# Interleaving the recurrent-gate quarters with the gate-branch products of a two-block kernel

## Chip, cores and metric

The kernel runs on one NeuronCore of a Trainium2 chip. The metric is the device time of one execution in microseconds (us).

## The reference

Two transformer-like blocks run one after the other over 256 tokens of width 1024. The change sits in the second block, in its recurrent branch. Cut to that branch, the second block computes:

```
xn = rmsnorm(x, norm_mix)
u_rnn, u_gate, q, k_c, v_c, ..., g_a, g_b = split(xn @ w_in)
xc = causal_depthwise_conv(u_rnn)                      # 1344 channels, 4 taps
r = sigmoid(block_diag(xc, w_a) + b_a)                 # 4 blocks of 336 channels
i = sigmoid(block_diag(xc, w_x) + b_x)
a = exp(-8 * r * softplus(-lam));  u = sqrt(1 - a^2) * (i * xc)
h_t = a_t * h_{t-1} + u_t                              # scan over tokens
y_a = h * gelu(u_gate)
y_b = sparse attention over q, k_*, v_*
h = x + (sigmoid(g_a) * (y_a @ proj_a) + sigmoid(g_b) * (y_b @ proj_b)) @ w_out
out = h + relu(rmsnorm(h) @ w_mlp_in)^2 @ w_mlp_out
```

All of it is in float32 precision: every weight and every activation is split into a high and a low part, and each product is made of three matmuls (high by high, high by low, low by high).

## The kernel before

**Products.** `ws` (L304 on) makes one product of 256 output channels by 256 tokens. Its weights come in two halves through `wload` (L284): one DMA from the SP queue into a `raw` tile (4 buffers), a cast on ScalarE (`whi`, L298, 3 buffers) and a subtraction on VectorE (`wlo`, L266, called from there, 3 buffers). Each half feeds 24 matmuls of 128x256, so a product has 48. It accumulates in one PSUM bank of the pool `acc`, which has 4 banks, and the bank is free again when the product's `sink` function has read it. `as_` (L327 on) makes products with tokens on the partitions: two banks, four weight pieces.

**The recurrent branch.** `block2` runs five products of `u_rnn` (`sink_u`) and one of the two 64-channel ends (`sink_t`). Each sink runs the four-tap convolution on VectorE (L1132 to L1135) and writes its 256 channels to a scratch tensor `sx` in HBM (L1142, L1147). The scratch is there because the convolution lies in rows of 128 channels and the block-diagonal gates want rows of 112: the quarters `xr` (3 rows of 112, 336 channels) are read back from `sx` (L1156). Both transfers are issued from ScalarE's queue.

Then `NY = 1` product of `u_gate` (`sink_ug`, L1151) is traced, and then the four gate quarters in a loop. A quarter splits `xr` (L274 on ScalarE, L275 on VectorE), loads two block-diagonal weights (`gate_a`, `gate_x`, each 112x1008), runs 54 matmuls into 3 banks, and passes the result through tanh, exp and tanh on ScalarE (L1177, L1179, L1184, L1186), a square on GpSimd (L1185), and short operations on VectorE (L1178, L1180, L1187). The other four products of `u_gate` follow the loop, then two products of the merge gates (`sink_g`, L1197, L1198).

After that comes the recurrence's tail: one square root over all 12 rows (L1201), a table load and a gelu over `u_gate`'s result (L1203), 12 multiplications (L1206) and 12 scans (L1207) on VectorE. The result is written to a scratch `sh` and read back in rows of 128 (L1209, L1215), multiplied (L1216) and split (L274, L275).

**The attention that follows** takes its tiles from pools that lie where the recurrent branch's pools (`rn`, `rn2`) lay. Its first product pair (`sink_c`, L1252 and L1253, two banks) writes the tile `zc`, and its first `as_` product (`sink_q`, two banks) comes behind.

**Order.** The kernel is scheduled by a list scheduler: each engine's queue is put in order before the run, by a timing model of its own and, among what that model holds ready, by the order in which the program was traced. On the chip each engine's queue then runs strictly in that order, and a transfer issued from ScalarE's queue waits there for what it reads.

Of the kernel before, what the change touches and what calls it, by code (L numbers as in the profile page):

```python
# [21 lines left out]
P = 128  # L22
T = 256
# [12 lines left out]
RW = 112  # L36
RC = 12
D_RNN = 1344
NX = 11
NH2 = 16  # L40
# [9 lines left out]
BG, BGH = 4, 5  # L50
KR = 2
NG1 = 2
NY = 1
RQ = lambda nc: nc.scalar
NL = 3
CHUNKS = (256, 256, 256, 128, 128)
# [8 lines left out]
FLEN = 512  # L65
# [153 lines left out]
class Kern:  # L219
# [875 lines left out]
    def block2(self):  # L1095
        nc, tc, a, cp = self.nc, self.tc, self.a, self.cp
        vec = self.vec
        w_in = ("w_in_2", 0)
        act = self.act_h
# [9 lines left out]
        HK = p1.tile([P, NH2, T], F32, name="HK")  # L1109
# [6 lines left out]
        with tc.tile_pool(name="rn", bufs=1) as rp, tc.tile_pool(name="rn2", bufs=2) as r2:  # L1116
# [3 lines left out]
            xr = rp.tile([RW, RC, T], F32, name="xr")  # L1120
# [7 lines left out]
            sx, sh = (self.dr.tile([D_RNN, T], F32, name=nm) for nm in ("sx", "sh"))  # L1128
# [9 lines left out]
            def sink_u(c, ps):  # L1138
                c *= 2
                for i in range(2):  # L1140
                    conv(c + i, P, ps[:, i])
                RQ(nc).dma_start(sx[c * P:(c + 2) * P].rearrange("(c p) t -> p c t", p=P), xc[:, c:c + 2, :])  # L1142

            def sink_t(c, ps):

                conv(NX - 1, half, ps[:half, 0])
                RQ(nc).dma_start(sx[(NX - 1) * P:D_RNN], xc[:half, NX - 1, :])  # L1147
                nc.vector.tensor_tensor(yg[half:, NX - 1, :], ps[half:, 0], rB[half:], op=ALU.mult)

            def sink_ug(c, ps):  # L1150
                nc.vector.tensor_tensor(yg[:, 2 * c:2 * c + 2, :], ps, rB2, op=ALU.mult)  # L1151
            for i in range(5):
                self.ws(w_in, 256 * i, 256, P, act, sink_u)
            self.ws(w_in, 0, 2 * half, P, act, sink_t, nkp=8, col="ends")
            for b in range(4):
                RQ(nc).dma_start(xr[:, 3 * b:3 * b + 3, :], sx[336 * b:336 * (b + 1)].rearrange("(c p) t -> p c t", p=RW))  # L1156
            for i in range(NY):
                self.ws(w_in, 256 * i, 256, P, act, sink_ug, base=D_RNN)
            nc.sync.dma_start(HK, bass.AP(tensor=self.scr.tensor, offset=self.scr.offset, ap=[[1, P], [FLEN, NH2], [1, T]]))
            for b in range(4):  # L1160
                xh = r2.tile([RW, 3, T], F32R, tag="xh", name=self.n("xh"))
                xl = r2.tile([RW, 3, T], F32R, tag="xl", name=self.n("xl"))
# [4 lines left out]
                for o in range(3):  # L1167
                    c = 3 * b + o
# [17 lines left out]
                nc.scalar.activation(W2[:, bs, :], W2[:, bs, :], AF.Tanh)  # L1186
                nc.vector.scalar_tensor_tensor(W2[:, bs, :], a2, 1.0, W2[:, bs, :], op0=ALU.add, op1=ALU.mult)  # L1187

            for i in range(NY, 5):
                self.ws(w_in, 256 * i, 256, P, act, sink_ug, base=D_RNN)  # L1190

            gate_out = [self.h8().rearrange("p (c t) -> p c t", c=8)]

# [17 lines left out]
            for c in range(0, NX, 2):  # L1211
                n = 2 if c < NX - 1 else 1
# [334 lines left out]
```

## Time and profile before

| What | Value |
|---|---|
| median of 3 runs | 1906.32 us (1904.04 to 1907.57) |
| profiled execution | 1909.29 us, of which the span is 1907.2 us |
| TensorE busy | 1614.0 us, 85% of the span |
| VectorE busy | 854.8 us, 45% |
| ScalarE busy | 577.0 us, 30% |
| recurrent branch of the second block | from about 1341 to 1456 us of the span |

The profiled execution is one run and 3.0 us above the median; 2.0 us of it lie outside its span. Times in the rows are microseconds from the start of the span.

### The profile page before, as it was taken

To read this page: it belongs to the slowest core of one execution; us is meant where nothing else is said; L and a number is where in the kernel's file an instruction comes from. 1 tells how busy PE (TensorE), PEld (TensorE's weight loads), DVE (VectorE), ACT (ScalarE), POOL (GpSimd) and SP (SyncE) were. 2 spreads that over 40 slices of the span, in tenths; PEclk is the share of its full clock that TensorE was granted. 3 is DMA by queue.
4 is the path that set the end of the run, shared out by engine and by line. 5 is a ranking of instruction groups with operands and counts; after the bars stand their busy time and mean duration, and the time that the engine had idled before them with its cause. 6 is when DMAs were issued, how large, how long until landed. Compare 5 with 4: busy or idle time off the path is not lost. (4 is left out here: it accounts for less than half of the span.)

```text
span 1907.2 us, 27940 instructions
## 1 busy us (share of the span) xinstructions
PE 1614.0 (85%) x11259; PEld 1082.4 (57%) x11259; DVE 854.8 (45%) x1760; ACT 577.0 (30%) x1033; POOL 60.1 (3%) x74
## 2 busy tenths in 40 slices
PE   8998887765667899988867766778999999999999
PEld 8898431221213698984311211136998788679987
DVE  7987220111001389862100110014888656556643
ACT  4455110001001345551100010014474445445532
POOL 0100000000000011000000000000011100000000
PEclk9999898887888999998988878789999999889999
DMA  7658899999999765598999999996657632226554
GB/s 281 226 176 302 334 425 427 426 425 425 426 427 426 299 249 187 178 330 351 426 426 427 424 427 426 427 425 257 203 172 251 203 112 91 80 89 189 196 190 133
DMA packets 109725, 567.27 MB, mean 297 GB/s; under 512 B 12107, under 2 KB 21259, under 8 KB 61713
## 3 DMA queue, kind: packets, MB, share of 16 engines
q1 hardware_dynamic: 102976, 558.45, 75.7%
q10 hardware_dynamic: 5984, 5.82, 1.0%
q8 instruction: 93, 1.52, 0.3%
q0 software_dynamic: 624, 1.09, 0.2%
q14 instruction: 48, 0.39, 0.1%
HBM read 561.48 MB, written 3.83 MB: 296 GB/s over the span
## 5 line engine op out<-in xcount | busy, mean ns | idle before, releaser
L261 PE MATMUL ps<-mw,h 128*32 128x512 f32 x2032 | 314.1, 718 | 139.7 <-DMA mw<-in_w_exp_up_dram 72.4
L266 DVE TENSOR_TENSOR wlo<-raw,whi 128x1024 fp32r<-128x1024 f32 (+3 forms) x286 | 343.5, 1203 | 187.6 <-ACT whi L298 180.0
L298 ACT CAST whi<-raw 128x1024 fp32r<-128x1024 f32 (+3 forms) x286 | 294.8, 1033 | 433.6 <-PE ps L261 211.3
L261 PE MATMUL ps<-h,whi 128*128 128x256 f32 x2208 | 295.0, 283 | 9.4 <-ACT h L407 6.3
L261 PEld LDWEIGHTS ps<-h,whi 128*128 128x128 f32 x2208 | 274.1, 190 | 15.7 <-ACT h L407 7.8
L261 PEld LDWEIGHTS ps<-mw,h 128*32 128x32 f32 x2032 | 50.0, 118 | 342.0 <-DMA mw<-in_w_exp_up_dram 164.5
L261 PE MATMUL ps<-mw,mw 128*32 128x512 f32 (+3 forms) x1584 | 145.4, 469 | 45.7 <-DMA mw<-in_w_exp_down_dram 40.1
L261 PE MATMUL ps<-h,wlo 128*128 128x256 f32 x1104 | 153.2, 280 | 0.5 <-DVE wlo L266 0.5
L261 PEld LDWEIGHTS ps<-h,wlo 128*128 128x128 f32 x1104 | 139.3, 188 | 1.2 <-DVE wlo L266 0.7
L904 DVE TENSOR_TENSOR x<-x,ps 128x512 f32<-128x512 f32 (+2 forms) x60 | 34.6, 581 | 225.7 <-PE ps L261 225.7
L839 ACT ACTIVATE mw<-ps 128x512 f32<-128x512 f32 x16 | 9.5, 597 | 399.4 <-PE ps L261 394.8
L840 DVE TENSOR_TENSOR mw<-mw,ps 128x512 f32<-128x512 f32 x16 | 11.0, 688 | 264.0 <-issue 139.6
L261 PEld LDWEIGHTS ps<-mw,mw 128*32 128x32 f32 (+1 forms) x1584 | 46.9, 115 | 128.9 <-DMA mw<-in_w_exp_down_dram 76.1
L501 DVE SCALAR_TENSOR_TENSOR mw<-mw,vec,mw 128x256 f32<-128x256 f32 x240 | 111.0, 508 | 0.0
L261 PE MATMUL ps<-whi,h 128*128 128x512 f32 (+1 forms) x512 | 104.0, 345 | 0.0
L261 PE MATMUL ps<-mw 128*128 128x512 f32 (+4 forms) x328 | 91.0, 446 | 14.8 <-ACT mw L898 14.3
L812 DVE TENSOR_TENSOR h<-ps,vec 128x256 f32<-128x256 f32 (+1 forms) x80 | 29.6, 371 | 161.4 <-PE ps L261 161.3
L261 PEld LDWEIGHTS ps<-h,h 128*128 128x128 f32 x512 | 68.3, 206 | 58.8 <-issue 52.0
L261 PEld LDWEIGHTS ps<-whi,h 128*128 128x128 f32 x512 | 78.9, 190 | 16.2 <-issue 3.8
L261 PE MATMUL ps<-h,h 128*128 128x128 f32 x512 | 78.7, 300 | 9.4 <-DVE h L800 9.4
L898 ACT COPY mw<-ps 128x512 f32<-128x512 f32 (+2 forms) x50 | 21.6, 431 | 205.3 <-PE ps L261 205.3
L261 PEld LDWEIGHTS ps<-mw 128*128 128x128 f32 (+1 forms) x328 | 46.1, 197 | 60.7 <-ACT mw L898 35.5
(338 smaller groups left out, 1809.7 us busy)
## 6 DMA issues: line engine op xcount, KB each, us to landing
mw<-in_w_exp_gate_dram SPq DMA_DIRECT2D x128, 1024.0 KB, 19.6
mw<-in_w_exp_up_dram SPq DMA_DIRECT2D x126, 1024.0 KB, 19.6
mw<-in_w_exp_down_dram SPq DMA_DIRECT2D x118, 1024.0 KB, 19.6
raw<-in_w_in_dram SPq DMA_DIRECT2D x129, 512.0 KB, 4.4
raw<-in_w_mlp_in_dram SPq DMA_DIRECT2D x32, 512.0 KB, 3.5
raw<-in_w_mlp_out_dram SPq DMA_DIRECT2D x32, 512.0 KB, 3.5
raw<-in_w_out_dram SPq DMA_DIRECT2D x24, 512.0 KB, 4.4
raw<-in_w_ple_gate_dram SPq DMA_DIRECT2D x16, 512.0 KB, 16.5
```

What stands on the lines that cost most here:

```text
L261: return self.nc.tensor.matmul(out, lhsT, rhs, start=start, stop=stop)
L266: self.nc.vector.tensor_tensor(lo, src, hi.bitcast(F32), op=ALU.subtract)
L298: nc.scalar.copy(hv, raw[ps, :n])
L501: nc.vector.scalar_tensor_tensor(cacc[:, c, :], u[:, c, j:j + T], vec[:, wc + j:wc + j + 1], cacc[:, c, :], op0=ALU.mult, op1=ALU.add)
L812: nc.vector.tensor_tensor(xg[:, k:k + n, :], ps[:, :n * P].rearrange("p (k s) -> p k s", k=n), self.vec[:, gcol + k:gcol + k + n].unsqueez ...
L839: nc.scalar.activation(sg, G, AF.Silu)
L840: nc.vector.tensor_tensor(sg, sg, U, op=ALU.mult)
L898: nc.scalar.copy(ys[i], Y[:, :dw])
L904: nc.vector.tensor_tensor(xs, xs, pc[:, :dw], op=ALU.add)
```

## The change

The constant `NY` goes. The read of a quarter of `xr` from `sx` moves from behind all six `u_rnn` products into a function `fetch`, which the sinks call: a quarter's read is traced right after the write that completes its 336 channels. In front of the first gate quarter stand two products of `u_gate` in place of one, and one more is traced behind each of the first three quarters; none follows the loop. The read of the position bias `HK` is traced ahead of these products and no longer behind the first. The number of products, matmuls, transfers and other instructions is the same.

```diff
-NY = 1
@@
                 RQ(nc).dma_start(sx[c * P:(c + 2) * P].rearrange("(c p) t -> p c t", p=P), xc[:, c:c + 2, :])
+                fetch((c + 2) * P)
+
+            def fetch(n):
+
+                while len(xps) < 4 and (len(xps) + 1) * 336 <= n:
+                    b = len(xps)
+                    RQ(nc).dma_start(xr[:, 3 * b:3 * b + 3, :], sx[336 * b:336 * (b + 1)].rearrange("(c p) t -> p c t", p=RW))
+                    xps.append(None)
@@
                 RQ(nc).dma_start(sx[(NX - 1) * P:D_RNN], xc[:half, NX - 1, :])
+                fetch(D_RNN)
@@
+            xps = []
             for i in range(5):
                 self.ws(w_in, 256 * i, 256, P, act, sink_u)
             self.ws(w_in, 0, 2 * half, P, act, sink_t, nkp=8, col="ends")
-            for b in range(4):
-                RQ(nc).dma_start(xr[:, 3 * b:3 * b + 3, :], sx[336 * b:336 * (b + 1)].rearrange("(c p) t -> p c t", p=RW))
-            for i in range(NY):
+            nc.sync.dma_start(HK, bass.AP(tensor=self.scr.tensor, offset=self.scr.offset, ap=[[1, P], [FLEN, NH2], [1, T]]))
+            for i in range(2):
                 self.ws(w_in, 256 * i, 256, P, act, sink_ug, base=D_RNN)
-            nc.sync.dma_start(HK, bass.AP(tensor=self.scr.tensor, offset=self.scr.offset, ap=[[1, P], [FLEN, NH2], [1, T]]))
             for b in range(4):
...
                 nc.vector.scalar_tensor_tensor(W2[:, bs, :], a2, 1.0, W2[:, bs, :], op0=ALU.add, op1=ALU.mult)
 
-            for i in range(NY, 5):
-                self.ws(w_in, 256 * i, 256, P, act, sink_ug, base=D_RNN)
+                if b < 3:
+                    self.ws(w_in, 256 * (b + 2), 256, P, act, sink_ug, base=D_RNN)
```

## Rows read from the trace of the kernel before

**Rows 1.** Page, part 1: busy us, share of the span, instructions of each engine.

```profile
PE 1614.0 (85%) x11259; PEld 1082.4 (57%) x11259; DVE 854.8 (45%) x1760; ACT 577.0 (30%) x1033; POOL 60.1 (3%) x74
```

**Rows 2.** Stages: length; busy us and instructions of PE, PEld, DVE, ACT, POOL; clock; DMA.

```profile
1372.90:1376.00 3.10, 0.04 (x1) 0.00 (x0) 2.74 (x6) 0.83 (x1) 0.00 (x0) 1.00 0.70 183
1376.00:1380.20 4.20, 3.78 (x18) 3.56 (x19) 3.37 (x5) 2.73 (x3) 0.00 (x0) 0.60 0.54 160
1391.00:1396.00 5.00, 3.32 (x26) 2.89 (x25) 3.17 (x4) 4.99 (x9) 1.47 (x1) 1.00 0.73 222
1406.80:1436.00 29.20, 29.20 (x249) 29.13 (x248) 27.93 (x45) 18.43 (x21) 3.64 (x2) 1.00 0.64 198
1372.90:1463.90 91.00, 84.55 (x645) 81.04 (x645) 82.41 (x127) 60.15 (x78) 9.73 (x10) 0.98 0.67 209
1419.80:1463.90 44.10, 43.24 (x320) 40.81 (x319) 41.98 (x63) 23.01 (x25) 3.12 (x6) 1.00 0.74 237
1466.00:1556.00 90.00, 90.00 (x568) 70.19 (x568) 57.63 (x129) 37.72 (x51) 11.26 (x9) 1.00 0.58 185
```

**Rows 3.** Waits of PE, 1338 to 1446: total us, times, longest.

```profile
PE ps L261 <- ACT xh L274: 3.1, 1, 3.1
PE ps L261 <- DVE wlo L266: 1.7, 2, 1.2
PE ps L261 <- ACT whi L298: 1.2, 3, 0.5
PE ps L261 <- DVE xl L275: 0.8, 2, 0.4
```

**Rows 4.** Timeline of PE: start, us, line, operands, count, idle before and releaser.

```profile
1371.84 1.10 PE L261 MATMUL ps<-h,wlo 128*128 128x256 f32 x8
...
1406.80 2.05 PE L261 MATMUL ps<-h,whi 128*128 128x256 f32 x16
...
1465.52 0.61 PE L261 MATMUL ps<-raw,zp 128*60 128x256 f32 x2 [0.48 <-PE ps L261]
```

**Rows 5.** Timeline of ACT and its queue (ACTq) around the first two quarters.

```profile
1363.94 0.38 ACTq L1142 DMA_DIRECT2D sx<-W  x1
...
1368.32 0.34 ACTq L1156 DMA_DIRECT2D xr<-sx  x1
...
1375.15 0.83 ACT L274 CAST xh<-xr 112x768 fp32r<-112x768 f32 x1 [4.91 <-DMA xr<-sx]
...
1377.73 1.03 ACT L298 CAST whi<-raw 112x1008 fp32r<-112x1008 f32 x1
1379.74 0.33 ACTq L1156 DMA_DIRECT2D xr<-sx  x1
1383.39 0.84 ACT L274 CAST xh<-xr 112x768 fp32r<-112x768 f32 x1 [4.63 <-DMA xr<-sx]
```

**Rows 6.** Timeline of the last quarter's way into the tail, ACT and DVE.

```profile
1411.99 0.85 ACT L1184 ACTIVATE Aa<-W 112x768 f32<-112x768 f32 x1 [0.50 <-DVE W L1178]
...
1416.91 2.77 ACT L1201 ACTIVATE W<-W 112x3072 f32<-112x3072 f32 x1
...
1419.86 2.77 DVE L1206 TENSOR_TENSOR ur<-ur,W 112x256 f32<-112x256 f32 x8
```

**Rows 7.** DVE's groups by line, 1419.8 to 1463.88: count, busy us, mean ns, idle before.

```profile
L266 DVE TENSOR_TENSOR wlo<-raw,whi 128x1024 fp32r<-128x1024 f32 x14 | 16.9, 1215 | 0.4 <-ACT whi L298 0.3
...
L1197 DVE TENSOR_TENSOR h<-ps,rB 128x512 f32<-128x512 f32 x2 | 1.4, 684 | 0.0
L1151 DVE TENSOR_TENSOR yg<-ps,rB 128x512 f32<-128x512 f32 x2 | 1.3, 670 | 0.0
```

**Rows 8.** Timeline of POOL and DVE where the attention's first tile is written.

```profile
1456.18 0.11 POOL L1246 MEMSET s<- 64x8 f32 x1 [41.44 <-DVE ya L275]
...
1462.57 1.30 DVE L1253 TENSOR_TENSOR s<-ps,rB 64x510 f32<-64x510 f32 x2
```

**Rows 9.** Timeline of the SP queue at the start of the recurrent branch.

```profile
1340.16 0.38 SPq L1159 DMA_DIRECT2D HK<-scr  x1
```

## The prediction

> **What bounds the kernel now.** I read the page first, then the stages around the change, then who TensorE waited for, then the queues one by one. The page says that TensorE is busy for 85% of the span [rows 1], so time is won where it stands still. The table of stages shows two such places in the recurrent gates: from 1372.9 to 1376.0 it does nothing, and from 1391 to 1396 it is busy for 3.32 of 5 us [rows 2]. The list of waits gives the sum: 3.1 us for `xh`, the first quarter's cast, and 1.7, 1.2 and 0.8 us for `wlo`, `whi` and `xl`, together 6.8 us [rows 3]. The first stand costs more than itself. Behind it the granted clock is 0.60 for 4.2 us, a mix of 1.2 and 2.4 GHz, and 18 matmuls ran [rows 2]; at the 0.117 us that one takes in the undisturbed stage (29.20 us for 249, [rows 2]) they are 2.1 us of work, and with the 0.4 us of standing in it the clock cost 1.7 us. What the change aims at is so 6.8 + 1.7 = 8.5 us, 0.45% of the span.
>
> The cause of the first stand is a round trip: the second `sx` write is issued at 1363.94, the read of quarter 1 at 1368.32, and its cast starts at 1375.15, 4.91 us after ScalarE was free for it [rows 5]. TensorE ended the one free product at 1371.84 + 1.10 = 1372.9 [rows 4].
>
> The Trainium skill, DMA: Bandwidth & Descriptors, section "Anatomy of one DMA — SWDGE (gpsimd) path", fits a transfer as 2.0 us and its bytes at 436 GB/s; an estimate by that page is 2.6 us for the write and 2.8 us for the read, so that quarter 1 would be there at 1369.3, before the free product ends, and there would be no stand to remove. The page's fit is for another issuing engine, this trace has 4.4 and 6.8 us, and the trace decides.
>
> **The change part by part.**
>
> *The reads of `xr`.* In the trace the first two reads stand already between the `sx` writes, not behind the last one [rows 5]: the scheduler had hoisted them to the moment their channels are written. Tracing them earlier gives them rank over casts, but nothing is ready sooner, since each waits for the convolution and the write before it. I take 0. Behind each read, ScalarE's casts are queued; a read put ahead of one cast more would hold it as the second one did, at most the 4.63 us of idle before the second `xh` [rows 5]. That is a rival below.
>
> *`HK`.* Its read is moved past two weight loads on the SP queue, but it is issued at 1340.16 already [rows 9], 33 us before TensorE ends the free product behind which it was traced. Cost 0 on either side: two loads that it might now hold up are needed 26 us later.
>
> *The second free product.* 48 matmuls by 0.117 us are 5.6 us, so TensorE is busy until 1378.5, past the 1375.15 at which the first quarter is there. The 3.1 us and the clock's 1.7 us go. What is late next is the quarter's own weights: there are 3 `whi` buffers, the second product now takes the two that `gate_a` and `gate_x` had, and ScalarE stands at `xh` until 1376.0. The next cast in its queue ran from 1377.73 to 1378.8 [rows 5], and the subtraction behind takes 1.2 us [rows 7], so the first low part is there at about 1380.0 and TensorE waits 1.2 us (it can do two matmuls of high parts before). Bounds: 0, if the cast goes ahead of the small gelu, and the rival's 5.4 us.
>
> *One product behind each of the first three quarters.* A quarter has 54 matmuls, 6.3 us of TensorE. ScalarE was busy for 4.99 of 5 us where TensorE waited from 1391 to 1396 [rows 2]: a quarter alone fills it. A product between gives it 5.6 us with two casts in them, so I let the 0.5 + 1.2 us of waits there go, and the small ones for `xl` as well; bounded by 0 and their 2.9 us in all.
>
> *What moves back: the last quarter.* Before, TensorE ended it at 1406.8 and four `u_gate` products followed [rows 4]. Now all stand ahead: 1372.9 + 4 x 5.63 + 4 x 6.33 + 1.2 = 1422.0. The tail needs the square root over all rows, hence the last quarter. From the last matmul to the first multiplication of the tail it took 1419.86 - 1406.80 = 13.1 us before, of which the part from exp on took 7.9 us [rows 4, 6]. The rest was ScalarE's arrears, which the mixing takes away. Between 8.7 us (7.9 and a tanh and a VectorE step) and 13.1 us I take 9, by the near end: the tail starts at about 1431 and not at 1419.9, 11 us later.
>
> *What waits for the tail.* The attention's first tile is cleared at 1456.18, after the last split of `ya`, for which GpSimd had stood 41.44 us [rows 8]: the attention's pools lie on the recurrent branch's and open when its last reader is done. Until then `sink_c` cannot empty its two banks, nor `sink_q` its two, and `acc` has four. Behind the first `as_` product TensorE has no bank. Before this was just in time: `sink_c` ended at 1463.87 [rows 8] and the next matmuls began at 1465.52, 0.48 us late [rows 4].
>
> VectorE does that stretch almost without a gap (27.93 of 29.20 us up to 1436, 41.98 of 44.10 us from the tail's start to the end of `sink_c`, [rows 2]). In these 1463.87 - 1419.86 = 44.0 us it did, beside the tail, 14 `wlo`, 2 `L1151` and 2 `L1197` [rows 7]. In the changed order TensorE is in the second `sink_g` product when the tail starts, so that 7 `wlo`, both `L1151` and one `L1197` are already done: 7 x 1.21 + 2 x 0.67 + 0.68 = 10.5 us, taken as 10, since neighbours overlap a little. So `sink_c` ends at 1431 + 34 = 1465.0, and with the 1.65 us that lay between, TensorE goes on at 1466.7 and not at 1465.5. **Sum: +1.2 us.** TensorE's work from 1431 to there is about 25 us out of 36: the 8.5 us that are saved in the gates come back as standing at the full banks or for `wlo` behind the scans, which are traced ahead of the `sink_c` products and so outrank their weights. A long stand may bring the slow clock again, up to 1.7 us; inside a stretch that VectorE sets it is hidden, so 0. From 1466 to 1556 TensorE is busy for 90.00 of 90 us [rows 2], and what is won or lost is kept.
>
> Bounds of the sum: no gap on VectorE (2.1 us were in the 44) and no late cast -2.1 us; ScalarE's arrears as before +4.1, the clock +1.7. The profiled execution of 1909.29 us would be 1910.5; against the median of 1906.32, **1907.5 us**, own range 1905 to 1914.
>
> **The rivals.**
>
> *The gates' gain is kept.* If the tail does not set the end, TensorE loses only the 1.2 us: -8.5 + 1.2 = -7.3, so 1899. For it: VectorE stands for 91.00 - 82.41 = 8.6 us between 1372.9 and 1463.9 [rows 2], and gelu can now run before the tail. Against it: 3 buffers stop `wlo` from running ahead, and the tail starts 11 us later. The Trainium skill, Perfetto Trace Analysis, section "Optimization Strategy" says that regimes bound by different engines may gain from being interleaved; that is this rival, and the trace bears it out for ScalarE in the gates only. A part of the gain, 4 us, is counted here.
>
> *ScalarE's queue stands at the second quarter (slower).* The second `xh` stood right behind one cast and the second read, and waited until 1383.39 [rows 5]. With a product more ahead of the quarters, the cast of the first quarter's second weight comes behind that `xh`, if the scheduler's model has quarter 2 early. Then it ends at 1385.3 and its low part at 1386.5; TensorE runs out at about 1381 and stands for 5.4 us. The last quarter, the tail and the banks all come that much later: +6.6, so 1912.9. It decides as soon as that one cast stands behind the second `xh`. For it: in the trace the second `xh` precedes even the first quarter's tanh. Against it: the cast is traced earlier and wins if both are ready.
>
> *The change does nothing*: the reads stood there already, and the scheduler keeps its order of products: 1906.3.
>
> **How the numbers follow.** Forecast 0.45, gain kept 0.20, ScalarE's queue 0.27, nothing 0.08. A change of 0.2%, 3.8 us, is about what a measurement of this kernel can tell from none. Faster by more: 0.22 (nearly all of the gain case, and a little of the forecast's low end). Slower by more: 0.32 (most of the queue case and the forecast's upper end). Between: 0.46. The range takes in the gain case's 1899 and the queue case's 1912.9: 1899 to 1914.
>
> **What the changed profile would show.** No wait for `xh` near 1373 and a clock of 1.0 behind it; quarters and products alternating on TensorE; the square root some 11 us later; TensorE standing for `wlo` between the scans or for a bank behind the first `as_` product; the clear of the attention's first tile near 1457 or later. If that clear comes at 1450 or before, the gain is kept and I am wrong; if TensorE stands for 5 us in the first quarter, the queue rival holds.

## The result, and the profile after

| What | Before | After |
|---|---|---|
| median, 15 executions of each beside one another | 1908.64 us (1902.04 to 1918.48) | 1921.83 us (1909.95 to 1930.59) |
| ratio after/before, 95% interval | | 1.0056 (1.0036 to 1.0076) |
| profiled execution, its span | 1909.29, 1907.2 us | 1925.15, 1923.2 us |

The change made the kernel slower: by the ratio 0.56%, some 10.7 us, with an interval of 6.9 to 14.5 us. The forecast was +1.2 us, its range ended at 1914, and its chance for "slower" was 0.32.

To see where the time came from, I measure each profiled execution from one point just ahead of the recurrent branch, the small product `ps<-dg,cst` on TensorE (1341.94 before, 1345.38 after; these 3.4 us arise in stages that the change doesn't touch). "Gates end" is the end of the last quarter's last matmul, "tail" the first multiplication of the recurrence's tail, "`sink_c` end" the end of the attention's first two sinks, "goes on" the matmuls behind them, the row `ps<-raw,zp` of [rows 4].

| us from the branch's start | Before | After | Forecast shift | Measured shift |
|---|---|---|---|---|
| gates end | 65.0 | 79.1 | +15.2 | +14.1 |
| gates end to tail | 12.9 | 12.9 | -4 | 0 |
| tail to `sink_c` end | 44.0 | 40.5 | -10 | -3.5 |
| goes on | 123.6 | 133.8 | +1.2 | +10.2 |
| the next stage, up to the softmax's first tile | 89.2 | 93.9 | 0 | +4.7 |

Behind that, the stage of the attention's softmax took 164.0 us before and 162.0 us after, and the last stage 188.4 and 188.2. So 3.4 + 10.2 + 4.7 - 2.0 - 0.2 = 16.1 us is the difference of the two spans (16.0); 14.9 us of it lie in the two stages at the change. These are two single executions; over all of them the difference is the 10.7 us above.

The busy time of the engines is nearly what it was [rows 1]. The page of the changed kernel, part 1:

```profile
PE 1615.2 (84%) x11259; PEld 1080.5 (56%) x11259; DVE 852.6 (44%) x1760; ACT 582.4 (30%) x1036; POOL 59.9 (3%) x74
```

TensorE's 1615.2 us of work are the same to 1.2 us, and what was added is standing. ScalarE has three instructions more, all of them table loads, since gelu and exp now alternate. Where the standing is, the windows of the changed kernel say (columns as in [rows 2]); the first is the gates, the second the way to the tail, the next four the tail:

```profile
1376.30:1424.30 48.00, 48.00 (x409) 48.00 (x408) 39.93 (x63) 38.89 (x53) 5.11 (x3) 1.00 0.70 216
1424.30:1437.40 13.10, 13.10 (x114) 13.10 (x113) 8.89 (x12) 12.69 (x14) 1.47 (x1) 1.00 0.58 188
1437.40:1452.00 14.60, 12.21 (x94) 11.55 (x93) 14.60 (x28) 6.95 (x8) 0.00 (x0) 1.00 0.49 158
1452.00:1457.20 5.20, 5.20 (x24) 4.20 (x23) 4.51 (x5) 1.36 (x2) 0.00 (x0) 1.00 1.01 321
1457.20:1463.20 6.00, 3.75 (x17) 2.68 (x15) 2.15 (x4) 1.13 (x2) 0.00 (x0) 1.00 0.93 354
1463.20:1472.00 8.80, 0.00 (x0) 0.00 (x0) 7.70 (x11) 4.68 (x7) 0.00 (x0) 0.56 0.42 120
1472.00:1479.10 7.10, 0.00 (x0) 0.00 (x1) 6.94 (x14) 1.19 (x2) 3.97 (x7) 0.50 0.31 92
1479.10:1484.60 5.50, 5.47 (x13) 3.77 (x14) 2.75 (x11) 0.00 (x0) 2.42 (x2) 0.50 0.00 0
1484.60:1574.00 89.40, 87.53 (x556) 68.08 (x555) 51.10 (x116) 36.36 (x48) 7.81 (x7) 1.00 0.51 168
```

In the gates TensorE is busy for 48.00 of 48 us at a clock of 1.00: all that [rows 3] held, and the slow clock of [rows 2], is gone. From 1461 to 1479 it does nothing at all, and behind that stand 13 matmuls run at a clock of 0.50, which is 1.2 GHz. The list of waits of TensorE from 1341 to 1485 (total us, times, longest) has only two entries where [rows 3] had four:

```profile
PE ps L260 <- issue: 18.2, 1, 18.2
PE ps L260 <- DVE wlo L265: 2.4, 1, 2.4
```

The four waits of the gates, 6.8 us, are gone; one of 18.2 us stands in front of the attention, and one of 2.4 us in the tail. What held it is on GpSimd's and TensorE's timelines of the changed kernel, the clear of the attention's first tile and the matmuls that go on:

```profile
1472.00 0.11 POOL L1253 MEMSET s<- 64x8 f32 x1 [40.84 <-DVE ya L274]
...
1479.13 1.08 PE L260 MATMUL ps<-raw,zp 128*60 128x256 f32 x2 [18.18 <-issue]
```

It is the same clear, behind the same last split of `ya`, as in [rows 8]; from it to the matmuls that go on it is 7.1 us, where before it was 9.3. The matmuls that go on read `zp`, which VectorE makes from `sink_c`'s tile. VectorE's rows, before:

```profile
1465.05 0.80 DVE L1284 TENSOR_SCALAR zp<-s,nv 128x60 f32<-128x60 f32 x4
```

and after:

```profile
1478.66 0.80 DVE L1291 TENSOR_SCALAR zp<-s,nv 128x60 f32<-128x60 f32 x4
```

In both TensorE goes on 0.47 us behind the start of this row. So what it stands for is this tile, and with it the end of `sink_c`; the prediction's full banks may hold it as well, but these rows don't show that.

### The profile page after: what moved, and what is told of

Read it like the earlier page. It is cut to its first block, busy times and chain, and to the rows that moved or that the text cites. A ratio compares the mean times of both kernels' runs of the same rounds, so it can differ in the third digit from the quotient of the medians.

```text
span 1923.2 us, 27939 instructions
## 1 busy us (share of the span) xinstructions
PE 1615.2 (84%) x11259; PEld 1080.5 (56%) x11259; DVE 852.6 (44%) x1760; ACT 582.4 (30%) x1036; POOL 59.9 (3%) x74
## 5 line engine op out<-in xcount | busy, mean ns | idle before, releaser
L260 PEld LDWEIGHTS ps<-h,whi 128*128 128x128 f32 x2208 | 275.6, 190 | 15.4 <-ACT h L406 7.9
L260 PE MATMUL ps<-mw 128*128 128x512 f32 (+4 forms) x328 | 88.2, 436 | 14.9 <-ACT mw L897 14.3
L260 PEld LDWEIGHTS ps<-h,h 128*128 128x128 f32 x512 | 67.2, 203 | 58.8 <-issue 53.6
```

The costliest lines, as they stand in the source:

```text
L260: return self.nc.tensor.matmul(out, lhsT, rhs, start=start, stop=stop)
```

## The experiments

Each order's marks, in us from the branch's start as above, from its profiled execution; the last column is what matters below.

| Kernel | Ratio to before (95%) | Gates end | Tail | `sink_c` end | Goes on | Gates end to `sink_c` end |
|---|---|---|---|---|---|---|
| before | 1 | 65.0 | 77.9 | 121.9 | 123.6 | 56.9 |
| after | 1.0056 (1.0036 to 1.0076) | 79.1 | 92.0 | 132.5 | 133.8 | 53.4 |
| e1 | 0.9997 (0.9975 to 1.0019) | 63.4 | 76.3 | 119.9 | 121.5 | 56.5 |
| e2 | 0.9981 (0.9961 to 1.0001) | 70.3 | 83.2 | 124.5 | 126.2 | 54.2 |
| e2b | 0.9989 (0.9967 to 1.0010) | 65.6 | 78.5 | 120.0 | 121.7 | 54.4 |
| e4 | 1.0029 (1.0014 to 1.0045) | 74.9 | 90.3 | 129.0 | 131.3 | 54.1 |
| e5 | 0.9998 (0.9978 to 1.0017) | 79.1 | 92.0 | 133.2 | 135.4 | 54.1 |
| e6 | 1.0025 (1.0002 to 1.0047) | 62.7 | 75.6 | 125.2 | 132.2 | 62.5 |
| e7 | 1.0013 (0.9997 to 1.0030) | 84.2 | 97.1 | 122.0 | 131.4 | 37.8 |
| e8 | 0.9997 (0.9969 to 1.0024) | 79.1 | 92.0 | 125.2 | 127.6 | 46.1 |
| e9 | 1.0032 (1.0008 to 1.0056) | 80.8 | 93.7 | 133.2 | 134.4 | 52.4 |
| e10 | 0.9997 (0.9974 to 1.0021) | 70.9 | 83.8 | 128.5 | 134.0 | 57.6 |
| e11 | 1.0031 (1.0010 to 1.0053) | 81.2 | 94.2 | 134.8 | 136.0 | 53.6 |
| e12 | 1.0017 (0.9998 to 1.0037) | 68.8 | 81.7 | 125.0 | 126.7 | 56.2 |
| e13 | 1.0065 (1.0041 to 1.0089) | 81.3 | 89.8 | 134.6 | 136.9 | 53.3 |
| e14 | 1.0046 (1.0026 to 1.0066) | 79.4 | 86.7 | 131.8 | 134.1 | 52.4 |
| e15 | 0.9964 (0.9942 to 0.9986) | 68.4 | 81.3 | 122.2 | 123.8 | 53.8 |
| e15b | 0.9987 (0.9964 to 1.0010) | 65.4 | 78.3 | 120.9 | 122.6 | 55.5 |

### Which part of the change does it

**e1: the reads alone.** The change's `fetch` and its place of `HK`, with the products in the old order.

```diff
-            for i in range(2):
+            for i in range(1):
...
-                if b < 3:
-                    self.ws(w_in, 256 * (b + 2), 256, P, act, sink_ug, base=D_RNN)
+                for i in range(*((1, 1), (1, 1), (1, 1), (1, 5))[b]):
+                    self.ws(w_in, 256 * i, 256, P, act, sink_ug, base=D_RNN)
```

> The reads of the quarters and of HK are traced where the change puts them; one product ahead of the first quarter, none between, four behind, as before. Theory (the tail starts late and the attention's first products stand at full PSUM banks): nothing changes, within 3 us of before, the last quarter ends as before and TensorE goes on behind the first query product about 92.6 us after the end of the first free product. Rival (the reads' higher rank holds ScalarE's queue): slower by most of the change's 10.7 us.

The ratio is 0.9997 and the marks are within 2.1 us of those of before. The reads and `HK` cost and give nothing, as forecast.

**e2 and e2b: two products ahead, none between, three behind.** The ranges in the last diff are `(2, 2), (2, 2), (2, 2), (2, 5)`, and two stand ahead. e2b is the same kernel once more.

> The change with two products ahead, none between the quarters, three behind the loop. Theory: the 3.1 us stand and the slow clock go (-4.8), but the last quarter comes one product (5.6 us) later, so the tail starts within 2 us of before and TensorE goes on at the same time: within 3 us of before. Rival (the gates' stands are the bound and only the mixing of the quarters costs): faster by about 5 us.

> The kernel of the run with two products ahead once more, in more rounds. From its profile (TensorE goes on behind the first query product 2.6 us later than before, and in slow clock) it should be 0 to 6 us slower than before; its first timing was 3.6 us faster with an interval that touches no change. If it is within 2 us of before, two ahead is worth nothing; if it is faster by 3 us again, the profile of one execution misleads.

3.6 and 2.1 us less than before in the timed comparisons, and both intervals hold 1. TensorE stood only 4.0 and 4.2 us in front of the attention. So the second product ahead isn't what cost the time. The two profiled executions show also how far one kernel's gates vary: they ended at 70.3 and 65.6, and TensorE waited 3.3 us for `xh` in the first and 0.2 us in the second. So a second product ahead doesn't always cover the round trip of `xr`; with the change's order no profiled execution shows that wait (after, e5, e8, e9, e11, e13, e14).

**e4: two ahead, one behind each of the first two quarters, one at the end.** The ranges are `(2, 3), (3, 4), (4, 4), (4, 5)`.

> Two products ahead, one behind each of the first two quarters, one behind the loop: the last quarter is one product earlier than in the change. Theory: the tail starts 5.6 us earlier than in the change and TensorE's stand of 18.2 us behind the first query product shrinks by about as much, to 11 to 14 us; slower than before by 4 to 7 us. Rival (the square root's and gelu's table loads on ScalarE set it, whatever the place of the quarter): as the change, +10 us.

1.0029: two of the three products between cost about half of what the change cost, 5.5 us of 10.7. With e2, the cost follows the number of products that stand between the quarters: 0, 2, 3 of them put the gates' end at 66 to 70, 75 and 79 us, and TensorE goes on at 122 to 126, 131 and 134 us. This is more than one order varies: the gates ended at 62.7 to 65.0 us in the three executions with the old order (before, e1, e6), and at 79.1 to 81.3 in the seven with the change's order and its buffers (after, e5, e8, e9, e11, e13, e14). e4's tail began only 1.7 us sooner than the change's, not the 5.6 expected, since gelu and its table load stand ahead of the root there.

### Does TensorE lack work, or is it kept from it

**e5: the change, with two merge-gate products more behind the gates.** `sink_g` products come from a pool of work that is otherwise done beside the attention.

```diff
-NG1 = 2
+NG1 = 4
```

> The change with four merge-gate products in place of two between the last quarter and the attention (two of the six that ran beside the attention's softmax move up). Theory: TensorE has 11.3 us more to do while the tail runs, so its 18.2 us stand shrinks to about 7 us plus what their weights add on VectorE, and the time is about that of before (within 4 us), unless the attention misses the two products. Rival (the stand is not a lack of free work, but ScalarE or VectorE are held by TensorE's own weights): the stand keeps its length, +10 us.

**e6: the kernel before with the same edit.**

> The kernel before with four merge-gate products in place of two ahead of the attention. Theory: the tail ends just in time in the kernel before, so two more products beside it save nothing there; what they do beside the softmax is lost or not: within 3 us of before. If slower by 5 us or more, these products were needed beside the softmax, and the change with four merge-gate products hides a larger gain than it shows.

**e10: the order of e2 with the same edit.**

> Two products ahead, none between the quarters, three behind, and four merge-gate products in place of two ahead of the attention. Theory: the last quarter is only one product late and the tail has two products more beside it, so the 4.0 us stand that two products ahead alone left behind the first query product goes too: 6 to 9 us faster than before. Rival (the two merge-gate products were needed beside the softmax): what is won is lost there, within 3 us of before.

In e5, TensorE's timeline shows the stand of 18.18 us at 8.38:

```profile
1475.27 1.08 PE L260 MATMUL ps<-raw,zp 128*60 128x256 f32 x2 [8.38 <-issue]
```

A wait of 2.50 us for a `whi` came in place of the 2.4 us for a `wlo`, and the ratio is 0.9998 where the change has 1.0056. The two products (96 matmuls, 11.3 us) fit into the stand, and the mark "goes on" hardly moved, 135.4 where the change has 133.8: it isn't set by TensorE's work. In e6 and e10, whose orders have little of such a stand without the edit (0.48 us in the kernel before, 4.0 us in e2), the same edit gave +4.8 us (e6) and no gain: 0.9997 for e10, where e2's order alone had 0.9981 and 0.9989. The 6 to 9 us that e10 was expected to gain didn't come. The two products had been cover where they were: in e6 TensorE was busy for 80.55 of the 86.01 us of the stage behind "goes on", before for 89.25 of 89.25. The change with this repair is where the kernel before is, not ahead of it: filling the stand gives back what it cost.

**e7: the attention's first tile in a buffer of its own,** so that its clear and `sink_c` don't wait for the recurrent branch's pool.

```diff
+        z8 = lambda dt: p1.tile([P, 2080], dt, tag="z8", bufs=1, name=self.n("z8"))
...
-            s8 = lambda dt=F32: sp_.tile([P, 2080], dt, tag="s8", bufs=4, name=self.n("s8"))
+            s8 = lambda dt=F32: sp_.tile([P, 2080], dt, tag="s8", bufs=3, name=self.n("s8"))
...
-            zc = s8()[:, :8 * (T + 1)].rearrange("p (v g t) -> p v g t", v=2, g=NG)
+            zc = z8(F32)[:, :8 * (T + 1)].rearrange("p (v g t) -> p v g t", v=2, g=NG)
```

(To make room, `xl` has one buffer and not two, and a later tile shares `z8`.)

> The change, but the attention's first tile lies in a buffer of its own that the recurrent branch doesn't use (it serves one of the two attention outputs later), and the low part of the quarters has one buffer in place of two. Theory: the first two attention products can be emptied before the recurrent branch's last reader, so TensorE has the second query product (10.7 us) to run before it stands at full banks: the 18.2 us stand is at most 9 us, and the time 7 to 12 us below the change, about that of before. Rival (TensorE waits for something other than the two banks, such as its weights): as the change, +10 us.

```profile
1478.28 1.08 PE L260 MATMUL ps<-raw,zp 128*60 128x256 f32 x2 [6.69 <-POOL hid L1271]
```

TensorE's row: `sink_c` ended 37.8 us behind the gates and no longer 53.4, TensorE went on 47.2 us behind them and no longer 54.7, and the ratio fell to 1.0013. The stand fell from 18.18 to 6.69 us, but only 2.4 us of that are an earlier end. The rest is that TensorE came to it later: the gates ended 5.1 us later, with 3.7 us of waits in them that the change doesn't have (its `xl` has one buffer less), and a wait for a `wlo` in the tail was 4.41 us and not 2.39. The second query product, which the theory had run ahead of the stand, still ran behind it. What remains is put down to `hid`, the next tile in the attention's pools; `zp` is in them too, and VectorE writes it right behind the last split of `ya`, which ended at 1477.19:

```profile
1477.23 0.97 DVE L1292 TENSOR_SCALAR zp<-z,nv 128x60 f32<-128x60 f32 x4
```

So the pools' opening is what the stand waits for: with `sink_c` out of the way, TensorE hangs on the last reader of the recurrent branch through the next tiles.

**e8: the change without the round trip of the tail's result through `sh`.** The product with gelu takes `xr` where it lies. It leaves out the branch's result (rows are multiplied with rows that don't belong to them).

```diff
-                if c % 3 == 2:
-                    RQ(nc).dma_start(sh[(c - 2) * RW:(c + 1) * RW]..., xr[:, c - 2:c + 1, :])
...
-                RQ(nc).dma_start(hs, sh[c * P:min((c + 2) * P, D_RNN)]...)
-                nc.vector.tensor_tensor(yg[p0:, cs, :], yg[p0:, cs, :], hs, op=ALU.mult)
+                nc.vector.tensor_tensor(yg[p0:RW, cs, :], yg[p0:RW, cs, :], xr[p0:, cs, :], op=ALU.mult)
```

> The change without the write of the scan's result to the scratch and its reading back: the multiplication with the gelu takes the scan's rows of 112 as they are, so the result of this branch is left out. Theory A (the tail is set by the round trip: 5.2 us for the last write and 6.0 us for the read behind the last scan, in which VectorE stands 5.6 us): the attention's first tile is cleared 8 to 12 us earlier and the time falls by as much, to that of before or below. Theory B (the prediction's: VectorE's work sets the tail): only VectorE's 5.6 us of standing can go, 3 to 5 us faster than the change.

GpSimd's and TensorE's rows:

```profile
1458.81 0.11 POOL L1250 MEMSET s<- 64x8 f32 x1 [31.29 <-DVE ya L274]
...
1469.34 1.08 PE L260 MATMUL ps<-raw,zp 128*60 128x256 f32 x2 [11.19 <-issue]
```

From the end of the scans to the clear it took 10.0 us in place of 20.1, TensorE stood 7.0 us less, and it went on 6.2 us earlier. The ratio, 0.9997, fell by more than that (11.3 us); the last section comes back to these executions. The round trip is about half of the way from the scans to the pool's opening; the other half is work on `ya`, with three `wlo` (3.7 us) between its pieces on VectorE.

### What sets the 12.9 us to the tail

From the last matmul of the gates to the tail I had taken 9 us. It took 12.9 before, after, in all of e1 to e12 but e4 (15.4), and in e15 and e15b. On ScalarE's timeline of the changed kernel the way is this, followed by GpSimd's and VectorE's part of it:

```profile
1423.34 2.11 ACT L297 CAST whi<-raw 128x1024 fp32r<-128x1024 f32 x2
1425.35 0.47 ACT L1184 ACTIVATE th<-ps,rv 112x256 f32<-112x256 f32 x1
1425.72 0.46 ACT L1186 ACTIVATE ur<-ps,rv 112x256 f32<-112x256 f32 x1
1426.40 1.05 ACT L297 CAST whi<-raw 128x1024 fp32r<-128x1024 f32 x1 [0.22 <-PE ps L260]
1427.47 1.28 ACT L1191 ACT_TABLE_LOAD   x1
1428.77 0.85 ACT L1191 ACTIVATE Aa<-W 112x768 f32<-112x768 f32 x1
...
1432.06 1.05 ACT L297 CAST whi<-raw 128x1024 fp32r<-128x1024 f32 x1
1433.13 1.28 ACT L1208 ACT_TABLE_LOAD   x1
1434.42 2.77 ACT L1208 ACTIVATE W<-W 112x3072 f32<-112x3072 f32 x1
...
1429.69 1.47 POOL L1192 TENSOR_TENSOR a<-Aa 112x768 f32<-112x768 f32 x1 [11.60 <-ACT Aa L1191]
...
1431.46 1.23 DVE L265 TENSOR_TENSOR wlo<-raw,whi 128x1024 fp32r<-128x1024 f32 x1 [0.60 <-ACT whi L297]
1432.61 0.95 DVE L1194 SCALAR_TENSOR_TENSOR W<-a,W 112x768 f32<-112x768 f32 x1
```

ScalarE is busy throughout, but not with the tail. A weight cast of a merge product stands in front of the last two tanh (1.05 us; the last matmul of the gates ended at 1424.47), another behind them (1.05), then exp's table (1.28). VectorE's last step, L1194, could have run when GpSimd's square was done at 1431.16; it stood behind a `wlo` that waited for a third cast, and began at 1432.61 (1.45). The root's table came behind a fourth, so that it ended 0.86 us after L1194. Added up, that is 5.7 us that aren't the tail's own.

**e9: gelu behind the root,** which takes exp's table load out of the way.

```diff
-            nc.scalar.activation(W2, W2, AF.Sqrt, scale=0.25)
+            sq = nc.scalar.activation(W2, W2, AF.Sqrt, scale=0.25)
...
-            nc.scalar.activation(yg[:, :NX - 1], yg[:, :NX - 1], AF.Gelu_apprx_tanh)
+            with tc.issue_after(sq.ins):
+                nc.scalar.activation(yg[:, :NX - 1], yg[:, :NX - 1], AF.Gelu_apprx_tanh)
```

> The change with the gelu over all rows queued behind the square root on ScalarE, as it was before. In the change gelu and its table ran among the last quarter's tanh, and the way from the last quarter's last matmul to the tail's first multiplication took 12.9 us, not the predicted 9. Theory A (gelu and the two table loads that it adds there make the difference): that way becomes 9 to 10 us, and the time is 2 to 4 us below the change. Theory B (the way's own steps): it stays at 12 to 13 us, and the time is as the change or, since the gelu now stands in the tail, up to 3 us above it.

Still 12.9 us, a miss for the idea that the table load was the length; the ratio's interval overlaps the change's. ScalarE's rows show who took the 1.28 us:

```profile
1427.83 1.05 ACT L297 CAST whi<-raw 128x1024 fp32r<-128x1024 f32 x1 [0.15 <-PE ps L260]
1429.50 0.63 ACT L1205 ACTIVATE h<-h 128x512 f32<-128x512 f32 x1 [0.62 <-DVE h L1204]
1430.66 1.05 ACT L297 CAST whi<-raw 128x1024 fp32r<-128x1024 f32 x1 [0.53 <-PE ps L260]
1431.73 1.28 ACT L1208 ACT_TABLE_LOAD   x1
```

The casts stand ahead of the root in the queue, and each waits until TensorE has used up a weight buffer. ScalarE came to them earlier and waited.

The last of these casts is what sets the 12.9 us. In e9 it begins at 1430.66, which is 7.58 us behind the gates' end; in the changed kernel at 1432.06, 7.59 us behind. The kernel before has it too, 7.58 us behind its gates' end at 1406.96:

```profile
1414.54 1.05 ACT L298 CAST whi<-raw 128x1024 fp32r<-128x1024 f32 x1
```

All 15 kernels with 12.9 us have it at 7.58 or 7.59, and in eight of them (e1, e2, e2b, e9, e10, e12, e15, e15b) the profile names TensorE as what it waited for. From its start the cast, the root's table load and the root take 5.3 us to the tail. So the pieces of the 5.7 us don't shorten the way one by one: what goes from ahead of this cast becomes waiting for TensorE.

**e11: the two merge products traced behind the tail's splits; e12: the same in the order of e2.**

```diff
-            for i in range(NG1):
-                self.ws(w_in, 256 * i, 256, P, act, sink_g, base=5296)
...
                 self.split(ya[0][p0:, cs, :], ya[1][p0:, cs, :], yg[p0:, cs, :])
+            for i in range(NG1):
+                self.ws(w_in, 256 * i, 256, P, act, sink_g, base=5296)
```

> The change with the two merge-gate products traced behind the recurrence's tail, so that square root, scans and splits outrank their weights' casts and subtractions. Theory (the 12.9 us from the last quarter's last matmul to the tail's first multiplication are held by the merge-gate casts in ScalarE's queue, some of which wait for TensorE): that way becomes 9 to 10 us, and the attention's first tile is cleared 3 to 6 us earlier; TensorE stands for weights earlier and at the banks for less, in sum 2 to 5 us faster than the change. Rival (the way's own steps set it): it stays at 12 to 13 us, and the time as the change or above it, since TensorE's two free products come later.

> Two products ahead, none between, three behind, and the two merge-gate products traced behind the tail. Theory: the tail starts no earlier than with two ahead alone by more than 1 us, since there are three products' weights ahead of it still, but it runs through faster; TensorE's stand of 4.0 us at the banks goes, and the time is 2 to 6 us below that of before. Rival (TensorE starves for weights under the scans): as before or up to 4 us slower.

Neither shortened the way (12.9 both times), nor the time by more than the intervals leave open. The list scheduler puts an operation that is ready into a queue's gap, whatever was traced ahead of it: the casts stood where they had stood.

**e13: ScalarE's part of the merge products forced behind the root; e14: gelu as well; e15: both, in the order of e2.**

```diff
-            for i in range(NG1):
-                self.ws(w_in, 256 * i, 256, P, act, sink_g, base=5296)
-            nc.scalar.activation(W2, W2, AF.Sqrt, scale=0.25)
+            sq = nc.scalar.activation(W2, W2, AF.Sqrt, scale=0.25)
+            with tc.issue_after(sq.ins):
+                for i in range(NG1):
+                    self.ws(w_in, 256 * i, 256, P, act, sink_g, base=5296)
```

> The change, with ScalarE's part of the two merge-gate products (four weight casts and two tanh) placed behind the square root in ScalarE's queue. Theory (the way to the tail is longer than forecast because casts of the merge products stand between the last quarter's steps): from the last matmul of the last quarter to the tail's first multiplication 9 to 10.5 us and no longer 12.9, TensorE stands at once behind the last quarter, and the merge products run beside the scans; the attention's first products come at the same time or up to 3 us earlier than in the change, so the time is between the change's ratio and 0.002 less (1.003 to 1.006). Rival (the tail's own steps set the 12.9 us): the way stays 12.9 us and the ratio rises by about 0.003 to 1.008, since TensorE stands for two products longer.

> As the run before, and gelu's activation and its table load behind the square root as well, so that the exp needs no table load between the last tanh and itself. Theory: the way to the tail is 1.3 us shorter again, 8 to 9 us, the forecast's value. Rival: 12.9 us as in all other runs. Time: 1.002 to 1.006 by the theory, 1.008 by the rival.

> Two free products ahead of the first quarter, none between, three behind, with the merge products' casts and gelu behind the square root. In this order only one or no merge product runs ahead of the tail, so the theory expects the way to be set by the casts of the u_gate products that stay, near 12 us, and the time to lie within 0.3% of the kernel without the two moves (0.998 to 1.001). The rival, that a shorter way by itself is worth its length, expects 9 us and a ratio of 0.996.

In e13 the way is 8.5 us, in e14 7.3: by 4.4 and 5.6 us shorter, where the rows above had 5.7 us of other work in it. ScalarE's rows of e13, and its first merge matmul on TensorE:

```profile
1422.40 0.48 ACT L1184 ACTIVATE th<-ps,rv 112x256 f32<-112x256 f32 x1 [1.28 <-PE ps L260]
1422.77 0.47 ACT L1186 ACTIVATE ur<-ps,rv 112x256 f32<-112x256 f32 x1
1423.26 1.28 ACT L1191 ACT_TABLE_LOAD   x1
1424.55 0.84 ACT L1191 ACTIVATE Aa<-W 112x768 f32<-112x768 f32 x1
...
1427.96 2.76 ACT L1206 ACTIVATE W<-W 112x3072 f32<-112x3072 f32 x1 [0.39 <-DVE W L1194]
...
1431.71 5.91 PE L260 MATMUL ps<-h,whi 128*128 128x256 f32 x32 [9.36 <-ACT whi L297]
```

The tail's own steps take less than the forecast's 9 us. And it gave nothing: TensorE goes on at 136.9 and 134.1 us where the change has 133.8, and the ratios of 1.0065 and 1.0046 are those of the change within their intervals. The merge products' four subtractions and two sinks on VectorE (4 x 1.2 + 2 x 0.69 = 6.2 us) now ran beside the scans, and from the tail's start to the end of `sink_c` it took 44.8 and 45.1 us in place of 40.5. TensorE's standing moved rather than went: in e13 it waited 14.2 us for `whi`, 1.0 for `wlo` and 3.3 in front of the attention, 18.5 in all, where the change has 20.6. e15 kept 12.9 us: there it is `u_gate`'s casts that stand in the way.

**e15b: e15 in more rounds,** since e15 came out 0.36% faster than the kernel before.

> The same kernel as e15_two_ahead_merge_gelu_behind, in more rounds. In that run's trace the stretch up to the attention's first products is as long as before (123.8 us from the branch's start, before 123.6) and the next stage 2.9 us longer; the stretch after those is 154.1 us at a clock of 0.93, where the kernel before has 164.0 us at 0.85. If the gain of 0.0036 is that stretch's clock in these executions alone, the ratio comes back nearer to 1 (0.998 to 1.001); if the changed order leads to the higher clock, it stays at 0.994 to 0.998.

0.9987, and the interval holds 1. With e2 and e2b four timings of orders with two products ahead and none between lie at 0.9964 to 0.9989, but e10 and e12, in that order too, at 0.9997 and 1.0017, and the mark "goes on" doesn't move in step with them (121.7 to 126.2). e15's interval alone leaves out 1. The mean granted clock over these four timings' executions was 0.911 to 0.914, beside 0.907 to 0.908 for the kernel before in the same comparisons, and 0.909 and 0.907 for e10 and e12. So the small gain goes with the clock, and why these executions had it isn't shown. I take it as not settled that any order here is faster than the kernel before.

## Why the prediction was wrong

The step that failed is the way from the gates' end to the end of `sink_c`. The forecast made it 9 + 34 = 43 us, from the kernel before's 57, by taking off ScalarE's arrears and 10 us of VectorE's work that would be done earlier, as if each of these were on the path; it took 53.4. The mark "goes on" was missed by 9.0 us: -1.1 in the gates, +4.0 up to the tail, +6.5 from there to the end of `sink_c`, -0.4 behind it. The slow clock behind the stand, put at 0, is most of another 4.7 us.

**The gates: right.** In the profiled execution all waits of the gates and the slow clock went: 48.00 of 48 us busy. The term for a late weight cast, 1.2 us, was not needed. The rival in which ScalarE's queue stands at the second quarter didn't come either. ScalarE's timeline of the changed kernel:

```profile
1376.78 0.84 ACT L273 CAST xh<-xr 112x768 fp32r<-112x768 f32 x1 [3.08 <-DMA xr<-sx]
...
1379.37 2.92 ACT L297 CAST whi<-raw 112x1008 fp32r<-112x1008 f32 x3
1382.48 0.84 ACT L273 CAST xh<-xr 112x768 fp32r<-112x768 f32 x1 [0.19 <-DMA xr<-sx]
```

Three weight casts went ahead of the second `xh`, which then waited 0.19 us where it had waited 4.63 [rows 5].

**The last quarter's shift: right.** Forecast 15.2 us later, measured 14.1; the late cast is the difference.

**From there to the tail: the term was mis-sized.** 9 us, measured 12.9. The step said that mixing takes ScalarE's arrears away and chose the near end of 8.7 to 13.1. The mixing did take away the arrears of the tanh, but the casts of the next products stayed in the queue, the last of them paced by TensorE at 7.6 us. With the casts behind the root the way is 8.5 us, and without gelu's table load 7.3 (e13, e14). I had costed ScalarE's work in the tail and not the queue that it stands in.

**From the tail to the end of `sink_c`: the term was mis-sized.** Forecast 34 us, measured 40.5. It was VectorE's work of 44 us less 10 us done earlier, taken without a gap. The window of the changed kernel from the tail's start to that end, and its part behind the scans:

```profile
1437.38:1477.90 40.52, 21.18 (x131) 18.45 (x129) 34.74 (x54) 15.34 (x19) 3.11 (x6) 0.83 0.59 193
...
1451.90:1472.00 20.10, 9.05 (x39) 6.96 (x37) 14.46 (x19) 7.28 (x10) 0.00 (x0) 0.81 0.73 243
```

VectorE's work was 34.74 us, as forecast. It did it in 40.5 us, because it was idle for 5.6 us behind the scans: 2.6 us for the reads of the round trip through `sh`, 2.1 for ScalarE's casts of what had been read, 0.8 for a weight cast. Before, other products' work had filled that wait. The window of the kernel before from the end of the scans to the clear:

```profile
1434.98:1456.18 21.20, 20.34 (x159) 19.48 (x159) 19.30 (x26) 15.37 (x18) 0.00 (x0) 1.00 0.87 292
```

It took 21.2 us with 19.30 us of work on VectorE, and 20.1 with 14.46 after; so the "10 us of work already done" was partly work that had cost nothing where it was. Whoever takes cover away from a latency doesn't shorten it. The chain of waits of the changed kernel (start, us, what) has the trip and what follows:

```profile
1451.93 5.22 DMA sh<-xr
...
1457.17 6.01 DMA ya<-sh
...
1465.54 3.49 DMA raw<-in_w_in_dram
...
1470.21 0.46 DVE wlo L265
...
1471.47 0.43 DVE ya L274
```

The write took 5.22 and the read 6.01 us, while the DMA engines, which also brought the weights of the next products, were busy for 1.01 and 0.93 of the time (windows above). Then the last split of `ya`, on which the pool hangs, stood in VectorE's queue behind a `wlo` whose weights had still to land. The Trainium skill, DMA: Bandwidth & Descriptors, section "Anatomy of one DMA — SWDGE (gpsimd) path", fits a transfer that GpSimd issues as 2.0 us and its bytes at 436 GB/s: an estimate by it is 2.8 us for the 344 KB of the write and 2.6 us for the 262 KB of the read. These rows, of transfers that ScalarE's queue issued, have about twice that; e8 prices the trip at 10.0 us of the way to the clear.

**The two together.** The last column of the experiments' table is steadier than any of its parts: from the end of the gates to the end of `sink_c` it took 52.4 to 56.9 us in every kernel that kept the round trip, the pool and two merge products, whether TensorE had 34 us of work there (after, by the windows above) or stood for 0.48 us behind it (before, [rows 4]), and whether ScalarE's casts were ahead of the root or behind it. So the mark moved with the gates' end: +14.1 - 3.5 = +10.6 us for `sink_c` and +10.2 for TensorE. The forecast had the mechanism (the gain comes back as standing in front of the attention) and had the column at 43 us.

What shortens the column is not the work that is taken from beside it. Counted by the products that are left between the gates' end and `sink_c` (those of `u_gate` and the merge products), it took, without e7 and e8: 62.5 us with eight (e6), 57.6 with seven (e10), 56.9 and 56.5 with six (before, e1), 53.8 to 56.2 with five (e2, e2b, e12, e15, e15b), 54.1 with four (e5) and with three (e4), and 52.4 to 53.6 with two (after, e9, e11, e13, e14). From six to two it gained some 3.5 us, where the forecast took off 14; from five down the column hardly moves, and only e7 and e8, which changed the tiles and the round trip, brought it to 37.8 and 46.1.

**The slow clock behind the stand: named and then set to 0.** I had bounded it by 1.7 us, as hidden under VectorE. It isn't hidden, since VectorE doesn't set the time behind the stand. 13 matmuls ran in 5.5 us at a clock of 0.50, half of it lost (2.7 us); then TensorE waited 1.0 us for a `whi` whose weights landed late and 0.6 us for another tile, in a stage that before had 90.00 of 90 us [rows 2]. Together these are 4.3 of the stage's 4.7 us.

**The rival that the gain is kept** rested on the Trainium skill, Perfetto Trace Analysis, section "Optimization Strategy", on interleaving regimes that are bound by different engines. The trace agrees for the gates alone (48.00 of 48 us busy), and the whole says otherwise (1.0056): the products that were interleaved were the next regime's cover. The sign that the prediction named for this rival, a clear at 1450 or before, didn't come either (1472.00).

## What to carry to other kernels

Before work is moved forward to fill a stand, measure the latency that it covers where it is: here 52 to 57 us from the last gate matmul to the end of `sink_c`, during which TensorE had 34 us of work in the changed kernel. A product moved ahead of such a chain delays it by its own length (5.6 us here) less the standing that it fills, and leaves a hole behind it. Other work put into that hole paid the loss back here and no more (e5). And the chain's own steps are costed in the queue that they stand in, with the casts of other products between them.

## What the runs showed of the hardware

The attention's softmax stage, the same 949 matmuls (to one) in every kernel but e5, e6 and e10, which have 923 to 925 there, took from 150.3 us (e4) to 165.5 us (e2) in the profiled executions of the others, at mean granted clocks of 0.94 and 0.84. The windows of that stage in the kernel before and in e15, each in its fence:

```profile
1554.80:1718.80 164.00, 156.39 (x949) 120.45 (x947) 96.06 (x302) 75.28 (x200) 0.00 (x0) 0.85 0.27 87
```

```profile
1557.00:1711.00 154.00, 145.65 (x949) 114.43 (x948) 95.70 (x302) 75.07 (x200) 0.00 (x0) 0.93 0.28 92
```

10 us between them with the same work on every engine: as much as the whole effect that this case is about. No edit here explains it. One kernel's executions differ by as much, and the mean granted clock of each execution goes with it: in e8 six took 1902 to 1905 us at 0.909 to 0.915, and four 1917 to 1918 us at 0.904 to 0.908; of the changed kernel's, the six at 0.909 or more took 1910 to 1917 us and the nine at 0.908 or less 1919 to 1931 us. In e7's ten executions no such order is seen. Which stage loses the time in an execution without a profile isn't shown, nor what makes one execution's clock differ from another's, so this stays open. It isn't what made the change slower: the changed kernel's executions had a mean clock of 0.908, as had those of the kernel before beside the experiments. This spread is why only ratios over many executions are used above, and why one profiled span against another would have misled: the profiled execution of e4 was 1906.58 us, below the median of the kernel before, and its ratio is 1.0029.
